# A transformer block on one core: output projection of all depth pairs as seven block products, weight sums from the prologue

## Chip, core and metric

The kernel runs on one core of a Trainium2 chip. Its engines are TensorE (PE; PEld is its weight load), VectorE (DVE), ScalarE (ACT), GpSimd (POOL) and SyncE (SP), which here only issues DMAs; each works through a queue of its own in the order of the program, and they wait for each other by semaphores. The metric is the device time of one execution in microseconds (us).

## The reference

One encoder block on x (1024 tokens by 1024, f32): a combined input projection, two groups of eight attention heads of width 64 (neighbourhood attention on a 16 x 64 grid with an 8 x 16 window and a relative bias; windowed attention with rotary positions, two key/value heads and a sink), SiLU gates, an output projection and a layer norm.

```python
h = jnp.einsum('bsd,de->bse', x, w_in[layer])
q_a, k_a, v_a, z_a, q_b, k_b, v_b, z_b = jnp.split(h, SPLIT_POINTS, axis=-1)
y_a = neighborhood_attention(q_a, k_a, v_a, rel_pos_bias[layer])
y_b = windowed_gqa_with_sink(rotary(q_b), rotary(k_b), v_b, sink_logits[layer])
mixed = jnp.concatenate([y_a * jax.nn.silu(z_a), y_b * jax.nn.silu(z_b)], axis=-1)
y = jnp.einsum('bse,ed->bsd', mixed, w_out[layer])
x = layer_norm(DEEPNORM_ALPHA * x + y, ln_gain[layer], ln_bias[layer])
```

## The kernel before

**Numbers.** Every operand of a product is held as two f16 tiles, hi and lo; a product is three passes, hi by hi, hi by lo, lo by hi. ScalarE makes hi (a scaled cast), VectorE or GpSimd makes lo (the source minus hi).

**Stages.** (1) Prologue, to about 60 us: v of both groups. A first half of the tokens is multiplied in f32 parts (line 551, eight depth steps; `load_wv` splits the weight, the last two steps' lo part on GpSimd, L510). `scales` (L573 to L584) then finds the scale `runit` of x and `unit` of the weight, by a chain of small VectorE operations. The second half of the tokens is done in f16: for each depth step k in the order `KO`, `ahead` lets ScalarE make the hi parts (L594 of the weight, L614 of x), VectorE the lo parts (`x16_part`, L615, and `wv_lo`, L598), three steps ahead of TensorE; two steps with the passes one after the other, the rest with all three passes of a matmul together. Steps take 2.45 us of TensorE. From the fourth on also the first half's x is split (`x16_part(0, k)`, again L615), which the input projection (`project`, L444) reads from 59.61 us on. Its weights are split by `w_split` (ScalarE L242, GpSimd L247 and L248). This part is written out in order by hand, so every queue has the order of the code. (2) Input projection and attention, to about 346 us: attention units with matmuls of the projection put between them, in step with a planner that gives the additional operations to GpSimd, ScalarE or VectorE by priority and estimated cost (`enq`, `fill_in`). Splits and sums of w_out and of the gated head outputs run here too. (3) Output projection and norm.

**The output projection.** The depth of 1024 is four pairs i = 0..3 of two 128-blocks, and the output tiles are taken as two halves of tokens (t and 4 + t) by two halves of columns. So there is a 2 x 2 by 2 x 2 block product for each pair. For pairs 0 and 1 (`NSP` = 2) it is done with seven products instead of eight, on sums S of the activations and T of the weights (`TERMS`: q1 = A11 B11, q2 = A12 B21, q3 = S4 B22, p4 = A22 T4, q5 = S1 T1, q6 = S2 T2, q7 = S3 T3). For pairs 2 and 3 it is eight plain products, appended to q2, q3, p4 and an eighth group d. The sums T of pairs 0 and 1 are made in stage 2 from loaded blocks of w_out (`t_prep`; `combine`, L1072 on GpSimd), split, and stored to a DRAM tile `td`, from which they are loaded when needed. Sums S come from `m_queue` and `m_split` (L1173, L1191).

**The end.** For each of four t, products are made into a PSUM bank and VectorE adds a bank to the f32 row tile `xr` (L1274; where the half row is complete, its statistics, L1280); `begin` and `finish` then take the row's mean and variance (L1284) and `norm` applies them. `norm` of tiles 0 to 2 and 4 to 6: ScalarE scales the whole row (L1346), GpSimd multiplies by the gain and adds the bias, in halves (L1348, L1349). Of tile 7 half is done by VectorE (L1339, L1343). The last tile is 3: its last product is cut in column blocks of 256, 128 and 128, and `norm_last` brings mean and deviation in through small matmuls (dm, L1311, and ds) while VectorE does the rest (L1315 to L1320). Warm-up matmuls without use (L1306) run between. GpSimd has nothing to do in the first half of the prologue but constants and L510.

**Heads.** As PSUM banks come free, the first closing products are put between the last attention units (`out_head`, `FILL_AT`, `FILL_N`), before all operands exist.

## Time and profile before

| | |
|---|---|
| time, median of 3 runs | 438.38 us (438.26 to 439.29) |
| the profiled execution: span from first to last instruction | 437.05 us |
| around the span, against the median | 1.33 us |
| granted TensorE clock | 1.000 |
| HBM read, written | 47.97 MB, 8.42 MB |
| prologue, to the first projection matmul | 59.61 us |
| first closing matmul (a head) | 346.05 us |
| last product ends, warm-up begins | 429.48 us |

The time of the profiled execution itself is its span of 437.05 us; the program's time has 1.33 us around it. Times in the rows are us from the start of the span. A row of a timeline has start, duration, engine, line of the program, operation, out<-in, and in brackets the idle time before it with what ended it; a row xN stands for N instructions in a run. A group has busy time, mean ns of one, idle time before.

### The profile page before, as it was taken

How to read it: one execution, taken by the hardware profiler on the slowest of the kernel's cores; microseconds unless marked ns; L12 is line 12 of the kernel's file. 1: busy time of each engine (PE TensorE's matmuls, PEld its weight loads, DVE VectorE, ACT ScalarE, POOL GpSimd, SP SyncE). 2: the span in 40 equal slices, each digit the busy share in tenths (PEclk: the TensorE clock that was granted, in tenths of full speed). 3: DMA queues.
4: the chain of work that ended last, by engine and by line, in shares of the span. 5: the costliest groups of instructions: out<-in, count | busy, mean ns of one | idle time of the engine just before them, and what ended most of it. 6: DMA issues, size and time to landing. Idle time of an engine off the chain costs nothing.

```text
span 437.0 us, 9409 instructions
## 1 busy us (share of the span) xinstructions
PE 431.1 (99%) x3225; PEld 253.3 (58%) x3225; DVE 337.6 (77%) x855; ACT 308.3 (71%) x663; POOL 275.6 (63%) x293
## 2 busy tenths in 40 slices
PE   9999999999999999999999999999999999999995
PEld 8997754444445656565656565565656555444444
DVE  5978976784878798888998898879887855575455
ACT  5749789768678979788988869887989743332321
POOL 0110073578428648778998899797899921068584
PEclk9999999999999999999999999999999999999999
DMA  8922479995429999997899999998999669711113
GB/s 265 406 92 61 119 242 324 255 291 175 128 56 196 207 181 205 163 191 129 153 190 215 189 204 191 226 196 159 182 191 247 118 125 370 300 48 73 73 73 121
DMA packets 128816, 80.09 MB, mean 183 GB/s; under 512 B 97280, under 2 KB 106368, under 8 KB 128768
## 3 DMA queue, kind: packets, MB, share of 16 engines
q1 hardware_dynamic: 128624, 79.36, 75.9%
q8 instruction: 25, 0.41, 0.4%
q14 instruction: 23, 0.19, 0.1%
q10 hardware_dynamic: 144, 0.13, 0.1%
HBM read 47.97 MB, written 8.42 MB: 129 GB/s over the span
## 4 chain that ended last, share of the span: by engine, by line
PE 79%; DVE 6%; ACT 6%; issue 4%; POOL 3%; DMA 1%; SPq 0%; DVEq 0%; ACTq 0%; POOLq 0%
PE ps_pj L444 39%; PE ps_s L1239 8%; PE ps_s L551 6%; PE ps_t L967 6%; PE ps_pj L1239 4%; PE ps_pj L551 3%; PE ps_t L551 3%; PE ps_s L890 3%; PE ps_s L891 3%; PE ps_t L1239 2%; POOL xr L1348 2%; POOL xr L1349 2%; DVE split L939 1%; ACT ps_s L920 1%; PE ps_t L1005 1%
## 5 line engine op out<-in xcount | busy, mean ns | idle before, releaser
L444 PE MATMUL ps_pj<-xf,wh 128*128 128x512 f16 x672 | 201.3, 379 | 0.0
L444 PE MATMUL ps_pj<-xf,wl 128*128 128x512 f16 x336 | 127.3, 379 | 0.0
L444 PEld LDWEIGHTS <-wh 128*128 128x128 f16 x672 | 63.7, 98 | 58.3
L920 ACT ACTIVATE ps_s<-sn,nm 128x321 f32<-128x321 f32 (+3 forms) x128 | 67.7, 529 | 33.4 <-DVE nm L904 32.3
L939 DVE SCALAR_TENSOR_TENSOR split<-ps_s,split 128x320 f16<-128x320 f32 (+2 forms) x128 | 62.7, 490 | 19.6 <-ACT split L938 18.3
L247 POOL TENSOR_SCALAR wr<-wr,wsc 128x512 f32<-128x512 f32 x32 | 22.9, 716 | 67.0 <-ACT wh L242 64.3
L938 ACT ACTIVATE split<-ps_s 128x320 f16<-128x320 f32 (+2 forms) x128 | 55.1, 430 | 1.7
L444 PEld LDWEIGHTS <-wl 128*128 128x128 f16 x336 | 32.8, 98 | 37.8
L248 POOL TENSOR_TENSOR wl<-wr,wh 128x512 f16<-128x512 f32 x32 | 40.3, 1260 | 2.7
L904 DVE CUSTOM_DVE_ANT_0 sn<-ps_s,bias,sg 128x368 f32<-128x368 f32 (+1 forms) x64 | 36.1, 565 | 3.5 <-PE ps_s L891 3.3
L904 DVE CUSTOM_DVE_ANT_0 sn<-ps_s,bm,nsk 128x320 f32<-128x320 f32 (+2 forms) x64 | 36.6, 572 | 2.6 <-PE ps_s L891 2.1
L890 PE MATMUL ps_s<-ks,qs 128*128 128x320 f16 (+3 forms) x128 | 38.2, 298 | 0.2 <-DVE split L939 0.2
L891 PE MATMUL ps_s<-ks,qs 128*128 128x320 f16 (+3 forms) x128 | 38.2, 298 | 0.0
L967 PEld LDWEIGHTS <-tr 128*128 128x128 f16 (+1 forms) x1056 | 36.2, 98 | 2.1 <-issue 0.4
L1239 PEld LDWEIGHTS <-m 128*128 128x128 f16 x198 | 19.0, 98 | 20.9 <-issue 0.2
L361 POOL COPY ks<-ks 64x512 f16<-64x512 f16 x40 | 25.9, 647 | 3.9 <-ACT ks L305 1.2
L1274 DVE SCALAR_TENSOR_TENSOR xr<-ps_s,yc,xr 128x512 f32<-128x512 f32 (+1 forms) x22 | 15.8, 724 | 13.8 <-PE ps_s L1239 13.5
L1346 ACT ACTIVATE xr<-xr,nmr,rstd 128x1024 f32<-128x1024 f32 x6 | 7.4, 1240 | 27.0 <-POOL nmr L1293 27.0
L1239 PEld LDWEIGHTS <-A 128*128 128x128 f16 x162 | 15.2, 98 | 15.7
L551 PEld LDWEIGHTS <-xf 128*128 128x128 f16 x192 | 18.6, 98 | 7.2
L242 ACT ACTIVATE wh<-wr,wsc 128x512 f16<-128x512 f32 x32 | 22.7, 709 | 0.0
L1348 POOL TENSOR_TENSOR xr<-xr,gb 128x512 f32<-128x512 f32 x13 | 16.9, 1302 | 8.1 <-ACT xr L1346 8.1
(223 smaller groups left out, 910.1 us busy)
## 6 DMA issues: line engine op xcount, KB each, us to landing
wr<-in_wt SPq DMA_DIRECT2D x32, 256.0 KB, 3.3
ws<-in_wt SPq DMA_DIRECT2D x15, 512.0 KB, 6.8
wor<-in_wo SPq DMA_DIRECT2D x20, 256.0 KB, 3.9
xr<-in_x SPq DMA_DIRECT2D x8, 512.0 KB, 10.4
out<-xr SPq DMA_DIRECT2D x15, 256.0 KB, 2.0
wob<-in_wo SPq DMA_DIRECT2D x14, 256.0 KB, 4.0
bias<-in_bias SPq DMA_DIRECT2D x8, 440.0 KB, 4.5
wvraw<-in_wv SPq DMA_DIRECT2D x9, 320.0 KB, 5.6
```

The costliest lines, as they stand in the source:

```text
L248: nc.gpsimd.tensor_sub(l, raw, h)
L361: nc.gpsimd.tensor_copy(place(t, o, half, col), place(t, a, half, col))
L444: nc.tensor.matmul(ps, a[:, k % 4, :], mv, start=(k == 0 and i == 0), stop=(k == KT - 1 and i == 2))
L551: nc.tensor.matmul(ps[:, :320], lh[:, ts], rh[:, cs], start=(k == ko[0] and i == 0), stop=(k == ko[-1] and i == 2))
L890: nc.tensor.matmul(ps[:, :n], q, sl[0], start=True, stop=False)
L891: nc.tensor.matmul(ps[:, :n], q, sl[1], start=False, stop=True)
L904: nc.vector.tensor_tensor_reduce(sn[:, at0:at0 + n], ps[:, :n], bias_t, sg[:, c:c + 1], init, op0=ALU.add, op1=ALU.min, accum_out=nm)
L920: nc.scalar.activation(pt[:, c], sn[:, c], AF.Exp, bias=nm, scale=-1.0, accum_out=acc)
L938: nc.scalar.activation(h, pt[:, c], AF.Copy, scale=PSCALE)
L939: nc.vector.scalar_tensor_tensor(l, pt[:, c], PSCALE, h, op0=ALU.mult, op1=ALU.subtract)
L967: nc.tensor.matmul(ps[:, w * m:w * m + e], a, b_, start=(i == 0), stop=(i == len(mms) - 1))
L1239: nc.tensor.matmul(ps[:, cs], lh[:, 128 * t:128 * t + 128], rh[:, cs], start=(fresh and e == 0 and n == 0), stop=(e == len(terms) - 1 and ...
```

## The change

It does all four depth pairs with the seven products and drops the plain ones (d, and the block B12). The sums T of all four pairs are made on GpSimd in the prologue: `t_load(i)` loads four 128 x 512 blocks of w_out into the tiles that held the f32 weight parts of v, `t_add(i)` makes four subtractions, `t_store(i)` stores the results in a DRAM tile `tf`. That is 4 MB more read and 4 MB more written in the prologue, all on SP's queue. `t_prep` in stage 2 loads tf, splits and stores, without subtractions; T of pairs 2 and 3 is loaded and split late (`t_late_load`, `t_late`), for which VectorE may take operations in the steps `LAST`. Sums S are made for pairs 2 and 3 too (`m_sums`, `m_last`). The heads have other lengths (`HEAD_N`: 9, 9, 6, 9, 9, 12, 12 matmuls instead of 12, 12, 6, 15, 18). The closing products have a new order; the last tile is 7, and its cut product is p4 with 12 matmuls a cut instead of q3 with 18. `norm` of every tile but the last is now split: ScalarE and GpSimd do half `ha`, VectorE does half `hb` with two operations (L1394, L1395 of the changed kernel). dm is made by ScalarE.

```diff
-NSP = 2
...
+T_KEYS = [("T1", 2), ("T1", 3), ("T2", 2), ("T2", 3), ("T3", 2), ("T3", 3), ("T4", 2), ("T4", 3)]
+T_SLOT = {"T1": 0, "T3": 1, "T4": 2, "T2": 3}
+T_AT, LAST = 122, range(129, 145)
...
+        wot = {}
+
+        def t_load(i):
+            for n in range(4):
+                t = vw.tile([128, 640], F32, tag=f"wv{'hl'[n % 2]}{2 * i + n // 2}", name="wot")
+                wot[i, n] = t[:, :512]
+                nc.sync.dma_start(wot[i, n], wo[i, :, n])
+
+        def t_add(i):
+            for o, a, b in ((0, 1, 0), (1, 3, 1), (3, 3, 0), (2, 2, 3)):
+                nc.gpsimd.tensor_sub(wot[i, o], wot[i, a], wot[i, b])
+
+        def t_store(i):
+            for n in range(4):
+                nc.sync.dma_start(tf[i, :, n], wot[i, n])
...
         nc.sync.dma_start(sk, sink)
+        t_load(0)
+        t_load(1)
+        t_add(0)
+        t_add(1)
...
+        t_store(0)
         wv_lo(KO[0])
         ahead(1)
         v_out(banks[4], 2, 0)
         ahead(2)
+        t_store(1)
+        t_load(2)
+        t_load(3)
+        t_add(2)
+        t_add(3)
...
+            if i == 5:
+                t_store(2)
...
         for i in range(4):
             sum_load(i)
+        t_store(3)
...
-    FILL_N = [48] * len(FILL) + [12, 12, 6, 15, 18]
+    FILL_N = [48] * len(FILL) + HEAD_N
...
-        def combine(o, a, b):
-            return enq("any", lambda eng: on_eng[eng].tensor_sub(wor[:, o], wor[:, a], wor[:, b]),
-                       *(t_sums[-1:] or [load_ops["wor", i, b] for b in range(4)]), prio=2, cost=SUM)
...
-        for n, t in ((0, t_sums[2]), (1, t_sums[1]), (3, t_sums[3]), (2, t_sums[3])):
+        for n in range(4):
+            t = enq("sp", lambda n=n: nc.sync.dma_start(wor[:, n], tf[i, :, n]), *([t_low[n]] if i else []))
...
+    def t_late_load(n, *deps):
+        key, i = T_KEYS[n]
+
+        def load():
+            t_raw[n] = wp.tile([128, 512], F32, tag="wr", name=f"tl{n}", bufs=5)
+            nc.sync.dma_start(t_raw[n], tf[i, :, T_SLOT[key]])
+
+        load_ops["tl", n] = enq("sp", load, *deps)
+
+    def t_late(n):
+        key = T_KEYS[n]
+
+        def hi():
+            if key not in part:
+                pair_of(big_ap([128, 2, 2, 512], F16, f"tp{n}"), *T_KEYS[n:n + 2])
+            nc.scalar.activation(part[key][0], t_raw[n], AF.Copy, scale=wsn)
+
+        o = enq("act", hi, load_ops["tl", n], prio=1.9, cost=0.65)
+        t_fin[n] = enq("any", lambda eng: lo_of(part[key][1], t_raw.pop(n), wsn, part[key][0], eng), o, prio=1.9, cost=LOW)
+        done[key] = [t_fin[n]]
...
-    NB = range(NSP, 4)
-    TERMS = {"q1": [("A11", "B11", n) for n in range(NSP)], "q6": [("S2", "T2", n) for n in range(NSP)],
-             "q5": [("S1", "T1", n) for n in range(NSP)], "q7": [("S3", "T3", n) for n in range(NSP)],
-             "q2": [("A12", "B21", n) for n in range(NSP)] + [(a, b, n) for n in NB for a, b in (("A11", "B11"), ("A12", "B21"))],
-             "q3": [("S4", "B22", n) for n in range(NSP)] + [(a, b, n) for n in NB for a, b in (("A11", "B12"), ("A12", "B22"))],
-             "p4": [("A22", "T4", n) for n in range(NSP)] + [(a, b, n) for n in NB for a, b in (("A21", "B11"), ("A22", "B21"))],
-             "d": [(a, b, n) for n in NB for a, b in (("A21", "B12"), ("A22", "B22"))]}
+    TERMS = {name: [(a, b, n) for n in range(4)] for name, a, b in (
+        ("q1", "A11", "B11"), ("q2", "A12", "B21"), ("q3", "S4", "B22"), ("p4", "A22", "T4"), ("q5", "S1", "T1"),
+        ("q6", "S2", "T2"), ("q7", "S3", "T3"))}
...
-            nc.gpsimd.tensor_scalar(dm, identf, mv[:, 0:1], -1.0, op0=ALU.mult, op1=ALU.mult)
+            nc.scalar.activation(dm, nident, AF.Copy, scale=mv[:, 0:1])
...
+            xr, ha, hb = xrs[t], slice(0, 512), slice(512, 1024)
             mv, sd = st_ or row_stats(t)
-            ha, hb = slice(0, 512), slice(512, 1024)
-            if t == 7:
-                nc.vector.scalar_tensor_tensor(xr[:, hb], xr[:, hb], mv[:, 0:1], gb[:, hb], op0=ALU.subtract, op1=ALU.mult)
-            rstd, nmr = row_scale(mv, sd, t == 7)
-            if t == 7:
-                nc.scalar.activation(xr[:, ha], xr[:, ha], AF.Identity, bias=nmr, scale=rstd)
-                nc.vector.scalar_tensor_tensor(xr[:, hb], xr[:, hb], rstd, bb[:, hb], op0=ALU.mult, op1=ALU.add)
-                nc.sync.dma_start(out[ts, hb], xr[:, hb])
-            else:
-                nc.scalar.activation(xr, xr, AF.Identity, bias=nmr, scale=rstd)
-            for h in (ha, hb)[:1 if t == 7 else 2]:
-                nc.gpsimd.tensor_mul(xr[:, h], xr[:, h], gb[:, h])
-                nc.gpsimd.tensor_add(xr[:, h], xr[:, h], bb[:, h])
-                nc.sync.dma_start(out[ts, h], xr[:, h])
+            rstd, nmr = row_scale(mv, sd)
+            nc.scalar.activation(xr[:, ha], xr[:, ha], AF.Identity, bias=nmr, scale=rstd)
+            nc.vector.scalar_tensor_tensor(xr[:, hb], xr[:, hb], mv[:, 0:1], gb[:, hb], op0=ALU.subtract, op1=ALU.mult)
+            nc.vector.scalar_tensor_tensor(xr[:, hb], xr[:, hb], rstd, bb[:, hb], op0=ALU.mult, op1=ALU.add)
+            nc.sync.dma_start(out[ts, hb], xr[:, hb])
+            nc.gpsimd.tensor_mul(xr[:, ha], xr[:, ha], gb[:, ha])
+            nc.gpsimd.tensor_add(xr[:, ha], xr[:, ha], bb[:, ha])
+            nc.sync.dma_start(out[ts, ha], xr[:, ha])
...
+        cb = [run("q5", t, bank("t"), range(3)) for t in range(2)]
+        q2(0, (3,))
+        add(1, 0, b[1])
+        q2(1, (3,))
+        q6(0)
+        for t in range(2):
+            run("q5", t, cb[t], (3,))
+            add(4 + t, 1, cb[t])
+        q7(0)
+        x_scale(2)
+        q3(0)
+        x_scale(6)
+        add(2, 0, b[2])
+        q6(1)
+        p4(0)
+        q5(2)
+        q7(1)
+        x_scale(3)
+        q3(1)
+        add(3, 0, b[3])
+        q6(2)
+        p4(1)
+        x_scale(7)
+        q5(3)
+        q7(2)
+        q2(2)
+        q3(2)
+        p4(2)
+        q6(3)
+        finish()
+        add(3, 1, run("q3", 3, cb[3]), whole=True)
+        q2(3)
+        run("q7", 3, b[3])
+        norm(3)
+        add(7, 1, b[3], whole=True)
+        norm_ahead(7)
+        add(7, 0, b[3])
         cuts = [((0, 256), bank("t")), ((256, 128), None), ((384, 128), None)]
         pn = bank("t")
         for c, ps in cuts:
             ps = ps or bank("pj" if c[0] == 256 else "s")
-            add(3, 1, run("q3", 3, ps, None, c), c, whole=True)
-        norm_last(3)
-
-    def m_last():
-        for n in ("A12", "A22"):
-            t = tiles["kq"].tile([128, 2, 512], F16, tag="ks", name=f"{n}_3", bufs=8)
-            part[n, 3] = t[:, 0], t[:, 1]
-        z = zt[ZP[3][1]]
-        for n, sl, eng in (("A12", ZL, "dve"), ("A22", ZH, "pool")):
-            m_split((n, 3), z[:, sl], low={eng: SUM[eng]})
-        need(*done["A12", 3], *done["A22", 3])
-
-    fill.extend((out_head((0,), range(4), "pj", "q2"), out_head((1,), range(4), "pj", "q2"),
-                 out_head((0, 1), (4,), None, "q2"), out_head((2,), range(5), "s", "q2"),
-                 out_head((0, 1, 2), range(2), "s")))
+            add(7, 0, run("p4", 3, ps, None, c), c, whole=True)
+        norm_last(7)
...
+    def m_last(between):
+        z, za = zt[ZP[3][1]], zt[ZP[3][0]]
+        need(*done["S3", 3])
+        for key in ("A12", "A22", "S1", "S2", "S4"):
+            m_home(key, 3)
+
+        def hi(key, src):
+            nc.scalar.copy(part[key, 3][0], src)
+
+        def lo(eng, key, src):
+            eng.tensor_sub(part[key, 3][1], src, part[key, 3][0])
+
+        hi("A12", z[:, ZL])
+        nc.vector.tensor_sub(za[:, ZL], z[:, ZH], za[:, ZL])
+        nc.gpsimd.tensor_add(za[:, ZH], za[:, ZH], z[:, ZH])
+        lo(nc.vector, "A12", z[:, ZL])
+        hi("S2", za[:, ZL])
+        hi("A22", z[:, ZH])
+        nc.vector.tensor_sub(z[:, ZL], z[:, ZL], za[:, ZL])
+        between()
+        lo(nc.vector, "S2", za[:, ZL])
+        lo(nc.gpsimd, "A22", z[:, ZH])
+        hi("S4", z[:, ZL])
+        lo(nc.vector, "S4", z[:, ZL])
+        hi("S1", za[:, ZH])
+        lo(nc.gpsimd, "S1", za[:, ZH])
```

GpSimd's queue in the prologue, from its last operation for v to its first splits of the projection weights; before:

```order
L510 TENSOR_TENSOR wvl_374<-wvraw,wvh_373 128x640
L510 TENSOR_TENSOR wvl_413<-wvraw,wvh_412 128x640
L247 TENSOR_SCALAR wr_520<-wr_520,wsc 128x512
L248 TENSOR_TENSOR wl_818<-wr_520,wh_817 128x512
L247 TENSOR_SCALAR wr_522<-wr_522,wsc 128x512
```

and of the changed kernel:

```order
L514 TENSOR_TENSOR wvl_375<-wvraw,wvh_374 128x640
L514 TENSOR_TENSOR wvl_414<-wvraw,wvh_413 128x640
L633 TENSOR_TENSOR wot<-wot 128x512 x16
L251 TENSOR_SCALAR wr_521<-wr_521,wsc 128x512
L252 TENSOR_TENSOR wl_883<-wr_521,wh_882 128x512
```

Sixteen subtractions (x16) stand between the lo parts of v's weight and the first split of a projection weight.

SP's queue from the last constant of the prologue on (sk is the sink); before:

```order
L231 DMA wr_528<-in_wt 128x512
L663 DMA bm<-in_bmask 128x320
L664 DMA sk<-in_sink 128x4
L591 DMA wvraw<-in_wv 128x640 x2
L604 DMA xraw_646<-in_xT 128x512
L604 DMA xraw_673<-in_xT 128x512
L604 DMA xraw_703<-in_xT 128x512
L604 DMA xraw_726<-in_xT 128x512
```

and of the changed kernel, from sk on:

```order
L684 DMA sk<-in_sink 128x4
L629 DMA wot<-in_wo 128x512 x8
L637 DMA tf<-wot 128x512 x4
L595 DMA wvraw<-in_wv 128x640 x2
L637 DMA tf<-wot 128x512 x4
L629 DMA wot<-in_wo 128x512 x8
L608 DMA xraw_703<-in_xT 128x512
L608 DMA xraw_730<-in_xT 128x512
L608 DMA xraw_760<-in_xT 128x512
L637 DMA tf<-wot 128x512 x4
L608 DMA xraw_787<-in_xT 128x512
```

The second loads of v's weight (wvraw) stand behind the first four stores, the second loads of x (xraw) behind eight stores and sixteen loads, one of them and the loads ws behind twelve stores; a store waits for its subtraction.

VectorE's queue near the end, around the norm of tile 7 before:

```order
L1280 BN_STATS stats_6037<-xr 128x6
L1274 SCALAR_TENSOR_TENSOR xr<-ps_s,yc,xr 128x512
L1280 BN_STATS stats_6037<-xr 128x6
L1284 BN_AGGR mv<-stats_6037 128x2
L1339 SCALAR_TENSOR_TENSOR xr<-xr,mv,gb 128x512
L1291 RECIPROCAL rstd<-sd 128x1
L1293 TENSOR_SCALAR nmr<-mv,rstd 128x1
L1343 SCALAR_TENSOR_TENSOR xr<-xr,rstd,bb 128x512
L1274 SCALAR_TENSOR_TENSOR xr<-ps_pj,yc,xr 128x512
```

and of the changed kernel, around the norm of tile 3, the one before the last:

```order
L1329 SCALAR_TENSOR_TENSOR xr<-ps_t,yc,xr 128x512
L1335 BN_STATS stats_6140<-xr 128x6
L1329 SCALAR_TENSOR_TENSOR xr<-ps_s,yc,xr 128x512
L1335 BN_STATS stats_6140<-xr 128x6
L1339 BN_AGGR mv<-stats_6140 128x2
L1346 RECIPROCAL rstd<-sd 128x1
L1348 TENSOR_SCALAR nmr<-mv,rstd 128x1
L1394 SCALAR_TENSOR_TENSOR xr<-xr,mv,gb 128x512
L1395 SCALAR_TENSOR_TENSOR xr<-xr,rstd,bb 128x512
L1329 SCALAR_TENSOR_TENSOR xr<-ps_s,yc,xr 128x512
L1335 BN_STATS stats_6185<-xr 128x6 x4
```

The two operations on SBUF halves that before stood only at tile 7 (xr<-xr,mv,gb and xr<-xr,rstd,bb) now stand in this way behind each of seven tiles, between additions from PSUM.

185 lines of the change are left out of this document (88 added, 97 removed).

## The prediction

> **What bounds the kernel now.** I read the page's busy shares first, then the waits of TensorE, then its chain of waits, then the timelines of single stretches. The busy shares and three rows of the page's slices:
>
> ```profile
> PE 431.1 (99%) x3225; PEld 253.3 (58%) x3225; DVE 337.6 (77%) x855; ACT 308.3 (71%) x663; POOL 275.6 (63%) x293
> ...
> PE   9999999999999999999999999999999999999995
> ...
> POOL 0110073578428648778998899797899921068584
> ...
> DMA  8922479995429999997899999998999669711113
> ```
>
> The waits of TensorE (what it waited for, total us, times, longest):
>
> ```profile
> PE ps_t L477 <- DVE warm L133: 1.0, 1, 1.0
> PE ps_t L1313 <- DMA out<-xr: 0.5, 1, 0.5
> PE ps_t L967 <- DVE z L992: 0.2, 1, 0.2
> PE ps_s L890 <- DVE split L939: 0.2, 1, 0.2
> ```
>
> TensorE waits 1.9 us in 437. Everything up to its last product is its own stream, so a matmul that goes is worth its pitch, and a wait that comes is paid in full. VectorE (DVE) and GpSimd (POOL) have spare time, but not everywhere: Each digit is the busy share of a slice of 10.9 us in tenths: GpSimd's idle slices are the 3rd to 5th (21.9 to 54.6 us) and those from 350 to 380 us. From the first of these the change takes its GpSimd time.
>
> **Part 1: fewer products.** In the chain of waits the pitch of the closing matmuls stands in one row (start, us, count):
>
> ```profile
> 401.00 10.37 PE ps_s L1239 x48
> ```
>
> 10.37/48 = 0.216 us for 512 columns. Per tile of 128 tokens the old terms are six per three-pass set: q1, q5, q6, q7 with 2 pairs (4 x 6 = 24), q2, q3, p4 with 2 + 4 terms (3 x 18 = 54) and d with 4 terms (12), 90 matmuls. New are seven products of 4 pairs by 3 passes, 84. Four tiles: 360 to 336, so 24 x 0.216 = **-5.2 us** of TensorE. The kept stages have no waits, so the eight POOL combinations that vanish from the attention stage (and two B splits) bring nothing themselves; it is their replacement that has a place of its own.
>
> **Part 2: sixteen subtractions on GpSimd in the prologue.** Before, GpSimd does nothing between two rows:
>
> ```profile
> 20.32 3.72 POOL L510 TENSOR_TENSOR wvl<-wvraw,wvh 128x640 fp32r<-128x640 f32 x2 [19.00 <-ACT wvh L507]
> 56.00 0.69 POOL L247 TENSOR_SCALAR wr<-wr,wsc 128x512 f32<-128x512 f32 x1 [31.96 <-ACT wh L242]
> ```
>
> and the same subtraction, in its old place, has this group:
>
> ```profile
> L1072 POOL TENSOR_TENSOR wor<-wor 128x512 f32<-128x512 f32 x8 | 10.2, 1272 | 0.4
> ```
>
> So 16 x 1.27 = 20.4 us fit into 32 us of idle GpSimd. The question is what they do to VectorE. Rows of the rotary part, where both engines work on SBUF (start, us):
>
> ```profile
> 110.60 0.68 DVE L381 TENSOR_TENSOR rp_sw<-rp_sw,sin 128x512 f32<-128x512 f32 x1
> 114.62 1.47 POOL L248 TENSOR_TENSOR wl<-wr,wh 128x512 f16<-128x512 f32 x1
> 115.00 1.64 DVE L381 TENSOR_TENSOR rp_sw<-rp_sw,sin 128x512 f32<-128x512 f32 x1
> 116.36 0.84 POOL L247 TENSOR_SCALAR wr<-wr,wsc 128x512 f32<-128x512 f32 x1 [0.27 <-ACT wh L242]
> 116.67 1.06 DVE L382 TENSOR_TENSOR rp_raw<-rp_raw,rp_sw 128x512 f32<-128x512 f32 x1
> ```
>
> Alone, L381 takes 0.68. At 115.00 it takes 1.64: it does its 0.68 after L248 has ended at 116.09. L247, issued at 116.36, waits for L381's end at 116.64 and ends at 117.20; L382, issued at 116.67, waits for that and ends at 117.73. The two engines take turns, whole instructions at a time. VectorE's operations in the prologue have the same two SBUF inputs:
>
> ```profile
> 28.28 0.15 DVE L580 TENSOR_TENSOR g<-g,least 32x2 f32<-32x2 f32 x1
> ...
> 35.02 0.75 DVE L615 SCALAR_TENSOR_TENSOR xf<-x,runit,xf 128x512 f16<-128x512 f32 x1 [1.36 <-ACT xf L614]
> 35.70 0.88 DVE L598 SCALAR_TENSOR_TENSOR wq<-wvraw,runit,wq 128x640 f16<-128x640 f32 x1
> 36.68 0.75 DVE L615 SCALAR_TENSOR_TENSOR xf<-x,runit,xf 128x512 f16<-128x512 f32 x1
> 37.35 0.88 DVE L598 SCALAR_TENSOR_TENSOR wq<-wvraw,runit,wq 128x640 f16<-128x640 f32 x1
> ...
> 57.94 0.92 DVE L615 SCALAR_TENSOR_TENSOR xf<-xraw,runit,xf 128x512 f16<-128x512 f32 x1
> ```
>
> and TensorE uses them at once (each of its eight steps takes 2.45 us; the third begins here):
>
> ```profile
> 38.37 0.57 PE L551 MATMUL ps_pj<-wq,xf 128*128 128x320 f16 x3
> ...
> 59.61 0.59 PE L444 MATMUL ps_pj<-xf,wh 128*128 128x512 f16 x2
> ```
>
> When do the subtractions come? The loads of wo stand behind these on SP; the page gives the time to landing of a load of that size:
>
> ```profile
> 18.09 3.00 SPq L231 DMA_DIRECT2D wr<-in_wt  x5
> ...
> 22.16 0.33 SPq L664 DMA_DIRECT2D sk<-in_sink  x1
> ```
> ```profile
> wr<-in_wt SPq DMA_DIRECT2D x32, 256.0 KB, 3.3
> ```
>
> At 0.6 us an issue the eight loads go out from 22.8 to 27.2 and land from about 27 to 31. A subtraction needs two tiles, so the first starts near 27.9, and GpSimd has eight in a row, 10.2 us if alone. Taking turns: L580 waits for the first (29.2 instead of 28.3). Subtractions 2 to 4 run beside small operations; then L615 and L598 of the first step, L615, L598 of the second and L615 of the third each let one through, 33.2 to 42.0, and the third step's L598 ends at 42.9 instead of 38.2. TensorE's third step then starts at 42.9 instead of 38.37: 4.5 us late. If loads land earlier or two of the pairings miss, one or two of the 1.27 us drop out; if VectorE always goes first, nothing is late. So 0 to 4.5; I take 3.2, the stepped value less one subtraction.
>
> The second eight wait on SP behind t_store(1), which waits for subtraction eight (41 us): 4 stores and 8 loads at 0.6 us, landing from about 46.5. They meet the last eleven L615/L598 up to the row at 57.94, which ended at 58.86 while its first reader (the tenth matmul of the projection, 59.61 + 9 x 0.216) came 2.9 us later. Eight subtractions are 10.2 us; maximum and scale operations and gaps of VectorE, which do not take part, hide 4 to 6. So 4 to 6 us of delay against 2.9 us of slack, which the first stall leaves as it is: 0 to 5, and I take 1.3, near the low end because GpSimd may run late instead. GpSimd cannot run much later, though: its own first split (56.00) waits for subtraction 16, and TensorE reads that split's lo half at 60.04 plus the delay. Sum of part 2: **+4.5** (0 to 9.5). The extra 8 MB themselves cost nothing: the DMA row of the slices shows 2, 2 and 4 tenths between 22 and 55 us; the x and ws loads that now stand behind the stores have several us to their readers.
>
> **Part 3: around the heads (346 to 372 us).** The order of TensorE is the same up to the first head. VectorE has spare time there, as the row before a late softmax scaling shows:
>
> ```profile
> 359.63 0.18 DVE L976 RECIPROCAL ri<-ps_t 128x4 f32<-128x4 f32 x1 [2.38 <-PE ps_t L967]
> ```
>
> A split of T and two splits of sums, three SBUF operations of 0.7 us each, now stand ahead of this reciprocal: 2.1 us into a gap of 2.38, less the time that GpSimd holds them up (one operation of 1.16, L248's length, at most). Between 0 and 1.5, I take one third of an operation: **+0.4**.
>
> **Part 4: the end.** Rows of VectorE at the end (start, us):
>
> ```profile
> 411.39 0.75 DVE L1274 SCALAR_TENSOR_TENSOR xr<-ps_s,yc,xr 128x512 f32<-128x512 f32 x1 [2.09 <-PE ps_s L1239]
> 412.18 0.69 DVE L1280 BATCH_NORM_STATS2 stats<-xr 128x6 f32<-128x512 f32 x1
> 412.79 0.15 DVE L1291 RECIPROCAL rstd<-sd 128x1 f32<-128x1 f32 x1
> ...
> 423.65 0.95 DVE L1339 SCALAR_TENSOR_TENSOR xr<-xr,mv,gb 128x512 f32<-128x512 f32 x1
> ...
> 424.84 1.44 DVE L1343 SCALAR_TENSOR_TENSOR xr<-xr,rstd,bb 128x512 f32<-128x512 f32 x1
> 426.20 0.74 DVE L1274 SCALAR_TENSOR_TENSOR xr<-ps_pj,yc,xr 128x512 f32<-128x512 f32 x1
> ...
> 430.47 0.37 DVE L1284 BATCH_NORM_AGGREGATE mv<-stats 128x2 f32<-128x48 f32 x1
> 430.88 0.75 DVE L1315 SCALAR_TENSOR_TENSOR xr<-xr,mv,gb 128x512 f32<-128x512 f32 x1
> ```
>
> An addition with its statistics takes 1.40 (411.39 to 412.79), an addition alone about 0.70. Before, six of eight norms cost VectorE only small operations. New, each norm puts two SBUF operations (0.75, start to start about 0.66, as L1315) on VectorE, beside GpSimd's multiply and add. From the end of q3 of tile 2 TensorE has 60 matmuls of 512, 12 of 256 and 24 of 128 columns left: 13.0 + 1.3 + 1.3 = 15.6 us. VectorE has behind that product: four additions with statistics (5.6), three additions alone (2.2), one statistics in four parts (0.8), three cuts of the last product with theirs (2.4), four aggregates (1.0), four reciprocals with nmr (1.2), together 13.2 us; and four norms of 1.32 alone (5.3), or, by the two rows at 423.65 and 424.84, which meet GpSimd's L1348 and L1349, at most 0.9 + 1.36 = 2.24 each (9.0). In the new order GpSimd's pair, 2.5 us, overlaps the next norm's first operation by some 0.5 us; I take 1.67 (6.7). So 19.9 against 15.6: VectorE becomes the bound there. TensorE, 5.2 earlier, ends q3 of tile 2 at 429.5 - 5.2 - 15.6 = 408.7 and VectorE's mean of the last tile is ready at about 409.1 + 19.9 = 429.0, the addition starting some 0.4 behind its product; it was 430.84. That is **-1.8** in place of -5.2 (-3.2 to +0.4 by the two bounds). The steps behind the mean are as before, dm on ScalarE may save 0.2, which I leave out.
>
> **Sum.** +4.5 + 0.4 - 1.8 = +3.1. The profiled execution spans 437.05, the median of the runs is 438.38, 1.33 more; 437.05 + 3.1 + 1.33 = 441.5.
>
> **Where the notes differ.** The Trainium skill, page "SBUF — State Buffer", section "Who interferes with whom", says that besides operations with two SBUF inputs also copy and tensor_scalar can enter modes that hold the pair of ports shared with GpSimd. For copies these rows agree (min/median/max ns: 228 alone, 1317 beside GpSimd); for small tensor_scalars they do not, L739 took 0.15 in the middle of a GpSimd operation:
>
> ```profile
> L751 DVE COPY vb<-vt x8: 228/229/1317, 68.1 to 82.3; 128x256 f16<-128x256 f16 x8
> ```
> ```profile
> 63.70 0.15 DVE L739 TENSOR_SCALAR vg<-vg 128x1 f32<-128x1 f32 x1
> ```
> ```profile
> 63.73 1.16 POOL L248 TENSOR_TENSOR wl<-wr,wh 128x512 f16<-128x512 f32 x1
> ```
>
> The chain of scales, L581 and four L583 behind L580, has two columns instead of one, so rows alone do not exclude that it waits.
>
> **Rivals.**
> - *VectorE keeps its pace in the prologue* (chance 0.27): it goes first whenever both are ready, or the subtractions fall into reduces and gaps, and GpSimd is the one that is late. For it: idle of 1.5 and 1.4 us before two L615. Against it: the turn at 116.36, and 10.2 us of GpSimd plus VectorE's L615/L598 do not fit before 38.2 from 27.9. It decides at a stall under about 1 us. Then 438.4 + 0.4 - 1.8 = 437.0, from 435.2 to 438.9 by the end's bounds: faster or no change.
> - *The whole gain* (0.10): also VectorE keeps up at the end because the order interleaves it better than I count, 438.4 - 5.2 = 433.2, up to 434.5.
> - *The scales wait as well* (0.13): each of five small operations behind L580 lets a subtraction through, runit comes up to 5 us later, of which 2 us are covered; 441.5 + 3 to 5, about 445.
>
> **How the numbers follow.** The forecast, stall of 2 to 7 us in the prologue, has 0.50 and gives 439.0 to 444.0, with some of the end's bounds 438.5 to 444.5. A measurement of this kernel tells about 0.3% (1.3 us) from no change. Faster: the whole gain 0.10, six tenths of the first rival 0.16, a small part of the forecast 0.04: 0.30. Same: the rest of the first rival 0.11 and 0.09 of the forecast: 0.20. Slower: 0.50. The range 434.5 to 446.0 leaves out most of the whole gain and the upper part of the last rival, under 0.2; the forecast's own range is 438.5 to 444.5.
>
> **What would show it.** Right: waits of TensorE on VectorE's lo splits between 33 and 50 us, VectorE's operations there 1.5 to 2.1 us long instead of 0.75 to 0.88, the first projection matmul at 63 to 66 instead of 59.61; in the end VectorE without idle from the q3 of tile 2 on, and warm matmuls starting earlier than the mean by more than 2 us. Wrong: the projection begins within 1 us of 59.61 (first rival), or VectorE waits for products up to the last cut (whole gain). The count of matmuls is certain, so a saving that is missing must show as idle time of TensorE.

## The result: slower, by about three times the forecast

| | before | changed |
|---|---|---|
| time, median | 438.6 us (438.26 to 439.29, 4 runs) | 449.5 us (448.2 to 452.57, 4 runs) |
| ratio of the times | | 1.0262, 95% interval 1.0221 to 1.0304 |
| profiled execution, span | 437.05 us | 446.4 us (its time 448.2) |
| last product ends | 429.48 us | 435.01 us |
| mean of the last tile ready | 430.84 us | 440.23 us |

The changed kernel is slower. Its 449.5 us lie outside the predicted range (434.5 to 446.0): the direction is right, the size is not. The profiled execution is 9.35 us longer than that of before, the medians differ by 10.9 us: the four runs spread more (448.2 to 452.6 us, with granted clocks of 0.992 to 0.985), and the profiled one is the fastest of them.

Busy shares and the clock row of the page of the changed kernel (tenths of full speed in 40 slices):

```profile
PE 428.9 (96%) x3189; PEld 249.8 (56%) x3189; DVE 357.4 (80%) x878; ACT 312.5 (70%) x676; POOL 292.5 (66%) x298
...
PEclk9999999999999999999999999999999999999996
```

TensorE has 36 matmuls less (18 whole ones, and six that were cut in three), as counted, but is busy 96% instead of 99%. What it waits for now (total us, times, longest):

```profile
PE ps_pj L1293 <- DVE xr L1329: 2.4, 1, 2.4
PE ps_t L1362 <- POOL xr L1354: 2.3, 1, 2.3
PE ps_pj L448 <- POOL wl L252: 1.6, 1, 1.6
PE ps_t L1368 <- ACT dm L1366: 1.2, 1, 1.2
PE ps_t L272 <- ACT junk L266: 1.0, 1, 1.0
...
PE ps_pj L555 <- DVE wq L602: 0.9, 2, 0.7
PE ps_s L923 <- DVE split L972: 0.8, 1, 0.8
PE ps_t L1000 <- DVE z L1025: 0.8, 1, 0.8
PE ps_s L555 <- DVE v L647: 0.8, 1, 0.8
```

Before, this view had four rows with 1.9 us in all. L555 and the wait of L448 for `wl` lie in the prologue, L272 at 94 us, L1000 and L923 in the attention, L1293 among the closing products, L1362 and L1368 behind the last product. To see what each costs, follow how much later than before the same instruction starts:

| instruction | before | changed | later by | added since |
|---|---|---|---|---|
| third matmul of the projection | 60.04 | 64.64 | 4.6 | 4.6 |
| `wm,ones` (L268, now L272) | 89.56 | 95.35 | 5.8 | 1.2 |
| last score matmul of the attention | 354.3 | 362.0 | 7.7 | 1.9 |
| last product, end | 429.48 | 435.01 | 5.5 | -2.2 |
| mean of the last tile, ready | 430.84 | 440.23 | 9.4 | 3.9 |
| span, end | 437.05 | 446.4 | 9.35 | 0.0 |

The -2.2 are 5.2 us of products that are gone, and 3.1 us of new waits at the closing products (2.6 at 383 us, 0.5 at 373 us).

**The prologue.** GpSimd's and VectorE's timeline of the changed kernel (start, us):

```profile
27.48 11.82 POOL L633 TENSOR_TENSOR wot<-wot 128x512 f32<-128x512 f32 x8 [4.06 <-DMA wot<-in_wo]
49.65 12.71 POOL L633 TENSOR_TENSOR wot<-wot 128x512 f32<-128x512 f32 x8 [10.35 <-DMA wot<-in_wo]
62.34 0.69 POOL L251 TENSOR_SCALAR wr<-wr,wsc 128x512 f32<-128x512 f32 x1
```
```profile
29.00 2.71 DVE L587 TENSOR_SCALAR unit<-g 32x2 f32<-32x2 f32 x4
...
33.42 1.25 DVE L619 SCALAR_TENSOR_TENSOR xf<-x,runit,xf 128x512 f16<-128x512 f32 x1 [1.51 <-ACT xf L618]
...
35.39 1.09 DVE L602 SCALAR_TENSOR_TENSOR wq<-wvraw,runit,wq 128x640 f16<-128x640 f32 x1
36.41 1.76 DVE L619 SCALAR_TENSOR_TENSOR xf<-x,runit,xf 128x512 f16<-128x512 f32 x1
38.09 1.89 DVE L602 SCALAR_TENSOR_TENSOR wq<-wvraw,runit,wq 128x640 f16<-128x640 f32 x1
39.90 0.74 DVE L619 SCALAR_TENSOR_TENSOR xf<-x,runit,xf 128x512 f16<-128x512 f32 x1
```

The first eight subtractions run back to back, and until GpSimd ends at 39.30 every lo part on VectorE takes 1.09 to 1.89 us instead of 0.75 to 0.88; behind that they are at their old length again, until the second eight begin. The second eight end at 62.3, and only then does GpSimd make its first split: TensorE's `wl` comes 1.6 us late.

**The end.** TensorE and VectorE of the changed kernel, from q3 of tile 2 on:

```profile
435.01 1.28 PE L1361 MATMUL ps_s<-warm 128*128 128x128 f16 x20
```
```profile
419.61 0.75 DVE L1329 SCALAR_TENSOR_TENSOR xr<-ps_t,yc,xr 128x512 f32<-128x512 f32 x1 [1.11 <-PE ps_t L1293]
...
421.32 0.74 DVE L1394 SCALAR_TENSOR_TENSOR xr<-xr,mv,gb 128x512 f32<-128x512 f32 x1
...
424.54 1.34 DVE L1394 SCALAR_TENSOR_TENSOR xr<-xr,mv,gb 128x512 f32<-128x512 f32 x1
425.91 1.64 DVE L1395 SCALAR_TENSOR_TENSOR xr<-xr,rstd,bb 128x512 f32<-128x512 f32 x1
...
439.86 0.37 DVE L1339 BATCH_NORM_AGGREGATE mv<-stats 128x2 f32<-128x48 f32 x1
```

VectorE has one wait of 0.42 us left between 419.61 and 440.23, 20.6 us; TensorE needs 15.6 us from the end of q3 (419.41) to its last product and has then to wait 5.2 us for the mean.

### The profile page after: what moved, and what is told of

It reads as the page before. It is cut to its first block, busy times and chain, and to the rows that moved or that the text cites. A ratio compares the mean times of both kernels' runs of the same rounds, so it can differ in the third digit from the quotient of the medians.

```text
span 446.4 us, 9462 instructions
## 1 busy us (share of the span) xinstructions
PE 428.9 (96%) x3189; PEld 249.8 (56%) x3189; DVE 357.4 (80%) x878; ACT 312.5 (70%) x676; POOL 292.5 (66%) x298
## 4 chain that ended last, share of the span: by engine, by line
PE 44%; DVE 19%; DMA 13%; ACT 10%; issue 8%; POOL 3%; SPq 2%; DVEq 0%; ACTq 0%; POOLq 0%
PE ps_pj L448 25%; PE ps_pj L1293 4%; PE ps_t L1000 4%; DMA vd<-vt 3%; PE ps_t L1293 3%; PE ps_s L1293 3%; DVE split L972 3%; DVE sn L937 3%; DMA wvraw<-in_wv 2%; PE ps_s L923 2%; PE ps_s L924 2%; POOL wot L633 2%; ACT ps_s L953 2%; DMA tl<-tf 2%; DMA T<-td 2%
## 5 line engine op out<-in xcount | busy, mean ns | idle before, releaser
L448 PE MATMUL ps_pj<-xf,wh 128*128 128x512 f16 x672 | 201.3, 379 | 0.0
L448 PE MATMUL ps_pj<-xf,wl 128*128 128x512 f16 x336 | 127.3, 379 | 1.6 <-POOL wl L252 1.6
L448 PEld LDWEIGHTS <-wh 128*128 128x128 f16 x672 | 63.8, 98 | 59.3 <-issue 1.3
L448 PEld LDWEIGHTS <-wl 128*128 128x128 f16 x336 | 32.9, 98 | 39.8 <-POOL wl L252 2.1
L923 PE MATMUL ps_s<-ks,qs 128*128 128x320 f16 (+3 forms) x128 | 38.2, 298 | 0.8 <-DVE split L972 0.8
L1000 PEld LDWEIGHTS <-tr 128*128 128x128 f16 (+1 forms) x1056 | 36.1, 98 | 2.7 <-issue 1.0
L633 POOL TENSOR_TENSOR wot<-wot 128x512 f32<-128x512 f32 x16 | 23.6, 1480 | 15.4 <-DMA wot<-in_wo 14.4
L1293 PEld LDWEIGHTS <-m 128*128 128x128 f16 x192 | 18.0, 98 | 22.2 <-issue 2.7
L1397 POOL TENSOR_TENSOR xr<-xr,gb 128x512 f32<-128x512 f32 x7 | 11.3, 1609 | 26.7 <-ACT xr L1393 26.7
L555 PEld LDWEIGHTS <-xf 128*128 128x128 f16 x192 | 18.6, 98 | 10.2 <-issue 3.0
L924 PEld LDWEIGHTS <-qs 128*128 128x128 f16 x128 | 12.5, 98 | 16.0 <-issue 1.5
L1393 ACT ACTIVATE xr<-xr,nmr,rstd 128x512 f32<-128x512 f32 x7 | 5.7, 813 | 22.2 <-DVE nmr L1348 22.2
```

The costliest lines, as they stand in the source:

```text
L448: nc.tensor.matmul(ps, a[:, k % 4, :], mv, start=(k == 0 and i == 0), stop=(k == KT - 1 and i == 2))
L633: nc.gpsimd.tensor_sub(wot[i, o], wot[i, a], wot[i, b])
L923: nc.tensor.matmul(ps[:, :n], q, sl[0], start=True, stop=False)
L924: nc.tensor.matmul(ps[:, :n], q, sl[1], start=False, stop=True)
L1000: nc.tensor.matmul(ps[:, w * m:w * m + e], a, b_, start=(i == 0), stop=(i == len(mms) - 1))
L1293: nc.tensor.matmul(ps[:, cs], lh[:, 128 * t:128 * t + 128], rh[:, cs], start=(fresh and e == 0 and n == 0), stop=(e == len(terms) - 1 and ...
```

## The experiments

All are timed in three rounds beside the kernel before, which had medians of 438.4 to 438.6 us there.

**The sums alone, and their transfers alone.** To the kernel before are added the loads, the subtractions and the stores of the prologue (`e1_before_sums`); the products stay as they were and the stored sums are not read. In `e2_before_moves` the subtractions are left out, and the raw blocks are stored. In `e3_after_nosubs` it is the changed kernel that lacks them, so that its T are raw blocks of w_out.

The edit of `e3_after_nosubs`:

```diff
         def t_add(i):
-            for o, a, b in ((0, 1, 0), (1, 3, 1), (3, 3, 0), (2, 2, 3)):
-                nc.gpsimd.tensor_sub(wot[i, o], wot[i, a], wot[i, b])
+            pass
```

> The kernel before with the prologue part of the change alone: the 16 loads of w_out blocks, the 16 subtractions on GpSimd and the 16 stores, at the places the change gives them; the results are not used, everything else is the kernel before. Theory (the two engines take turns at SBUF, and late loads follow): the first projection matmuls are 4 to 5 us late, the reads of the projection weight sums near 90 us 1 us more, so the span is 437 + 5 to 6 = 442 to 443. Rival 1 (the prologue costs little, the change loses its time at the end): 437 to 438.5. Rival 2 (the loss in the attention stage comes from here as well, by transfers that come late): 444 to 445.

> As the run with the prologue part alone, but without the 16 subtractions: loads and stores of w_out blocks only, the stored blocks are the raw ones and not used. Theory (the subtractions hold up VectorE's lo parts): the projection starts within 0.5 us of 59.6, the span is 437 to 438.5, and what it has over 437 is the wait near 90 us. Rival (transfers in SyncE's queue hold up the second loads of x and of v's weight): the projection starts 2 us late or more, span 440 to 443.

> The changed kernel without the 16 subtractions: the weight sums T are the raw blocks of w_out. Theory: TensorE is not late at the start of the projection, 4.6 us of the changed kernel's 446.4 go, span 441 to 442. If the wait near 90 us goes as well: 440.5. Rival (the prologue's delay is made up by later slack or returns as another wait): 444 to 446. The waits of the attention stage (1.0 us near 208 and 1.0 near 260) and the ones at the end (2.4 near 383, 3.9 behind the last product) stay by the theory.

Measured: 445.31 us (ratio 1.0159, 1.0135 to 1.0184), 439.98 us (1.002, 0.9997 to 1.0043) and 443.96 us (1.0142, 1.0107 to 1.0177). Waits of TensorE in the kernel before with the sums:

```profile
PE ps_pj L445 <- POOL wl L249: 1.7, 1, 1.7
PE ps_pj L552 <- DVE wq L599: 1.2, 2, 0.7
...
PE ps_s L552 <- DVE v L644: 0.8, 1, 0.8
...
PE ps_pj L552 <- DVE xf L616: 0.6, 1, 0.6
```

None of these rows is there with the transfers alone. So the 8 MB more cost between nothing and 1.9 us by the interval, and the subtractions 5.3 us (445.31 less 439.98): the prologue's part of the theory holds, in a kernel that has nothing else of the change. (The forecasts are spans, 442 to 443, 437 to 438.5 and 441 to 442; the traces have 443.8, 438.5 and 441.9, so the first is 0.8 too low.) But without the subtractions the changed kernel is still 5.5 us slower than the one before, although it has 5.2 us fewer products. So some 10.7 us, up to 1.9 of them by the transfers, are lost outside the sums, of which the prediction had 3.8 (3.4 at the end, 0.4 at the heads).

**Half of the sums.** As `e1_before_sums`, with only the first eight subtractions.

```diff
-            for o, a, b in ((0, 1, 0), (1, 3, 1), (3, 3, 0), (2, 2, 3)):
+            for o, a, b in ((0, 1, 0), (1, 3, 1), (3, 3, 0), (2, 2, 3))[:4 if i < 2 else 0]:
```

> The kernel before with the prologue part, of which only the first eight subtractions are left (pairs 0 and 1); loads and stores all stay. Theory (the first eight hold up the lo parts of the first steps, the second eight GpSimd's own first split): TensorE loses 2.5 to 3.5 us between 33 and 42 us and nothing near 63; span 441 to 442.5. Rival (either eight cost about the same, by total port time): 439.5 to 440.8.

Measured: 443.01 us (1.0095, 1.0067 to 1.0123). TensorE's gaps between 33 and 42 us (the time from start to start beyond the usual pitch) add up to 2.7 us (3.5 with all sixteen, 3.0 in the changed kernel), and the wait for `wl` at 63 us is gone. So the first eight cost 2.7 to 3.5 us, the second eight 1.7 us in TensorE's wait: the forecast had 3.2 and 1.3.

**What holds VectorE: reading or writing?** In the place of each subtraction, three memsets on GpSimd in the kernel before: it writes for as long, but reads nothing.

```diff
-                nc.gpsimd.tensor_sub(wot[i, o], wot[i, a], wot[i, b])
+                for _ in range(3):
+                    nc.gpsimd.memset(wot[i, o], 1.0)
```

> The kernel before with the loads and stores of the prologue part, and in place of each of the 16 subtractions three memsets of the same tile on GpSimd: GpSimd is busy in the same places and waits for the same loads, but reads no SBUF. Theory (VectorE's operations with two inputs and GpSimd's reads take turns): VectorE's lo parts keep their 0.75 and 0.88 us, the projection starts within 0.7 us of 59.6, span 438 to 439.5. Rival (any operation of GpSimd there holds VectorE up, or the waits between the queues do): the projection 2 us late or more, span 441 to 444.

Measured: 442.21 us (1.0084, 1.0056 to 1.0112). GpSimd and VectorE:

```profile
27.19 13.11 POOL L631 MEMSET wot<- 128x512 f32 x24 [3.34 <-DMA wot<-in_wo]
```
```profile
29.41 2.21 DVE L584 TENSOR_SCALAR unit<-g 32x2 f32<-32x2 f32 x4
...
33.33 0.75 DVE L616 SCALAR_TENSOR_TENSOR xf<-x,runit,xf 128x512 f16<-128x512 f32 x1 [1.51 <-ACT xf L615]
...
34.80 0.88 DVE L599 SCALAR_TENSOR_TENSOR wq<-wvraw,runit,wq 128x640 f16<-128x640 f32 x1
```

Beside 13 us of memsets the operations with two SBUF inputs keep 0.75 and 0.88 us, so it is GpSimd's reading that holds them up. The tensor_scalars of the scales do not keep their length: four of them took 0.68 us before, and take 2.21 us here and 2.71 us beside the subtractions. This is what the Trainium skill states, page "SBUF — State Buffer", section "Who interferes with whom", and the prediction set aside on the row of L739, which has 128x1. By the Trainium skill, page "VectorE: DVE Perf Modes", section "Mode 2×_2P — use both read ports for one tensor", such a mode needs an outermost dimension longer than one that is even (or odd and alike in source and destination), which 32x2 has and a single column has not. The measurements agree with both. The row of L739 shows less than the prediction read from it: it starts at 63.70, 0.03 us ahead of GpSimd's operation, not in the middle of one. Rows of the changed kernel do show it: four tensor_scalars of 128x1 between 50.23 and 50.88 us take 0.15 to 0.20 us each, while GpSimd's first subtraction of the second eight runs until 51.26.

The time of this run lies between the theory and its rival: the profiled execution spans 441.3 us (438 to 439.5 by the theory). The scales alone make `runit` 2.0 us late, the projection begins at 60.65 instead of 59.61, and GpSimd's first split, which stands behind the memsets, holds TensorE up for 1.3 us more.

**The same sums behind the prologue.** Half of them on VectorE, from 65 us on, with three edits of experiments below in it (casts, pools, norm share).

```diff
+            at(26 + 7 * n, t_add, n // 4, n % 4, nc.gpsimd)
+            at(29 + 7 * n, t_add, 2 + n // 4, n % 4, nc.vector)
```

> The changed kernel with the casts and the pools mended (the norm as changed), and the 16 subtractions moved behind the prologue: loads as in the changed kernel, eight subtractions on GpSimd and eight on VectorE, one every 1.5 us between the matmuls of the first projection (65 to 77 us), stores there too. Theory (the place of the subtractions is what costs, not their number): TensorE is not late at 59.6 us, the splits that the projection needs have slack of several us there; span 439 to 440.5, against 446.4 less 1.2 and 1.2 with the subtractions in the old place. Rival (GpSimd's splits of projection weights, or v's parts, are now late): 442 to 445.

Measured: 457.99 us (1.0443, 1.042 to 1.0467), the slowest of all. The prologue has no gap, but the operations of the projection are late instead:

```profile
PE ps_pj L448 <- POOL wl L252: 8.5, 1, 8.5
PE ps_t L272 <- ACT junk L266: 4.9, 1, 4.9
```

TensorE's stream has no slack there either, and the granted clock is 0.50 for 3.4 us behind the wait of 4.9 us and for 10.2 us around the one of 8.5 us (see the last section). As the edits are mixed in this kernel, the shares of the sums and of the pools in these 13.4 us are not separated.

**The wait at 94 us.** L272 waits for a reduction on ScalarE. ScalarE is held up by a copy `rp_raw` of the rotary part (L382), which waits 4.1 us for stores `vd<-vt`. The full diff, beyond the excerpt shown, takes these scratch tiles (tag `va`) from another pool, `kq` instead of `ap`; there they come to lie on the v tiles, whose stores must end first. The experiment makes this move alone, in the kernel before (the line below, and the two like it for the other tiles of this tag).

```diff
-        raw = tiles["ap"].tile([128, 1024], F32, tag="va", name="rp_raw", bufs=6)[:, :512]
+        raw = tiles["kq"].tile([128, 1024], F32, tag="va", name="rp_raw", bufs=6)[:, :512]
```

> The kernel before with one part of the change: the scratch tiles named va (the rotary's raw and swapped tiles, the gathered v, the biases) are taken from the pool kq instead of ap, nothing else. Theory (the first rotary tile then lies on v tiles that are still being stored, and ScalarE waits for those stores): a wait of TensorE of 1 to 1.6 us for the weight sums (L268) near 88 us, ScalarE's L378 there with an idle time ended by the stores of v; span 438 to 438.7. Rival (that wait belongs to the prologue's extra transfers): no wait there, 437 to 437.3.

Measured: 439.66 us (1.003, 1.0012 to 1.0048, ten runs). ScalarE and the waits of TensorE in it:

```profile
89.09 0.60 ACT L378 ACTIVATE rp_raw<-ps_pj 128x512 f32<-128x512 f32 x1 [5.63 <-POOL wl L248]
```
```profile
PE ps_t L268 <- ACT junk L262: 1.7, 1, 1.7
```

and the same instruction in the changed kernel (without the subtractions it waits 4.10 us for the same stores):

```profile
94.09 0.60 ACT L382 ACTIVATE rp_raw<-ps_pj 128x512 f32<-128x512 f32 x1 [4.12 <-DMA vd<-vt]
```

In the kernel before this copy begins at 85.87, with the product that it reads. The move alone brings a TensorE wait of 1.7 us to the kernel before, whose view of waits had none there, and from the third matmul of the projection to the last score matmul this trace takes 1.6 us more (295.9 instead of 294.3). So that the move causes the wait is shown. What the copy waits for is read from the views, which name the last of several things: a store in the changed kernel, GpSimd's split in this run.

**The wait at 383 us.** q7(0) needs the bank that VectorE's addition (0, 1) reads. Rows of ScalarE, VectorE and TensorE of the changed kernel:

```profile
375.26 1.06 ACT L1324 ACTIVATE xr<-xr 128x1024 f32<-128x1024 f32 x1 [5.26 <-DMA xr<-in_x]
376.22 0.60 ACT L1505 CAST A<-z 128x512 f16<-128x512 f32 x1
```
```profile
376.86 0.69 DVE L1508 TENSOR_TENSOR A<-z,A 128x512 f16<-128x512 f32 x1 [1.58 <-ACT A L1505]
...
384.95 0.73 DVE L1329 SCALAR_TENSOR_TENSOR xr<-ps_pj,yc,xr 128x512 f32<-128x512 f32 x1
```
```profile
385.74 1.46 PE L1293 MATMUL ps_pj<-T,m 128*128 128x512 f16 x6 [2.43 <-DVE xr L1329]
```

The addition ends at 385.68, and q7(0) starts at 385.74. The casts for the last sums stand on ScalarE behind the scaling of x, which waits for its load. The experiment puts them ahead of it.

```diff
-        x_scale(0)
...
-        m_last(lambda: add(0, 0, b[0]))
+        m_last(lambda: (x_scale(0), add(0, 0, b[0])))
```

> The changed kernel with one order changed on ScalarE: the scaling of row tile 0 of x, which waited 5.3 us for its load, stands behind the first three casts of the last pair's sums instead of ahead of them. Theory (those casts stand behind a late load, and so VectorE reaches the addition that TensorE's q7 of tile 0 waits for 1.6 us late): the wait of 2.4 us near 383 shrinks to about 1, span 1 to 1.6 less than the changed kernel's 446.4 if the end follows, 444.8 to 445.4. Rival (VectorE's own two-input operations beside GpSimd's make the wait, not the casts): 446 to 446.6, no change.

Measured: 448.31 us (1.0234, 1.0191 to 1.0277), against 449.5 us; the two intervals overlap. The wait before q7(0) falls from 2.59 to 1.61 us (start to start beyond the usual pitch). But q6(0), ahead of it, now starts 0.4 us late, because the addition of tile 0 comes later in this order, so the stretch loses 2.0 us instead of 2.6. By this one trace about a quarter of the loss is the order on ScalarE; the rest stands in VectorE's own queue, which in this trace is busy from 382.24 up to the addition without a pause, and ahead of that has a lo part and a sum of 1.74 and 1.54 us instead of 0.69:

```profile
379.00 1.74 DVE L1507 TENSOR_TENSOR A<-z,A 128x512 f16<-128x512 f32 x1
380.78 1.54 DVE L1515 TENSOR_TENSOR z<-z,z 128x512 f32<-128x512 f32 x1
```

That GpSimd's share of those last sums is the rest of the cause is read from this, not tested by itself.

**The end: less of the norm on VectorE.** Of each row VectorE does 256 columns instead of 512, ScalarE and GpSimd 768.

```diff
-            xr, ha, hb = xrs[t], slice(0, 512), slice(512, 1024)
+            n = 512 if t == 3 else 768
+            xr, ha, hb = xrs[t], slice(0, n), slice(n, 1024)
```

> The changed kernel, with another share of the norm of tiles 0 to 2 and 4 to 6: VectorE does 256 columns instead of 512, ScalarE and GpSimd 768 instead of 512 (GpSimd in pieces of 384). Theory (VectorE is the bound from q3 of tile 2 on, 20.6 us of work beside 15.6 of TensorE): three of the four norms in that stretch lose 2 x 0.33 us each and meet GpSimd more often, the mean of the last tile is ready 1.5 to 2 us earlier against TensorE's last product (5.2 us behind it before, 3.2 to 3.7 now), span 444.4 to 445. Rival (GpSimd's longer work holds VectorE up as much as it saves, or the end waits for GpSimd): 446 or more.

Measured: 448.77 us (1.0233, 1.0198 to 1.0268). VectorE's stretch from q3 of tile 2 to the mean is 20.5 us (418.87 to 439.35), as long as before the edit (20.6). The halved operations of the first of these norms take 0.48 us; those of the next two do not:

```profile
423.26 0.89 DVE L1395 SCALAR_TENSOR_TENSOR xr<-xr,mv,gb 128x256 f32<-128x256 f32 x1
424.19 1.10 DVE L1396 SCALAR_TENSOR_TENSOR xr<-xr,rstd,bb 128x256 f32<-128x256 f32 x1
...
426.26 1.13 DVE L1395 SCALAR_TENSOR_TENSOR xr<-xr,mv,gb 128x256 f32<-128x256 f32 x1
```

GpSimd, which has half more columns, is busy then, and VectorE waits for a turn. What it saves in columns it pays in turns: the rival of this experiment was right.

**The end: the norm as before.** ScalarE and GpSimd do whole rows, and the addition and the statistics of tile 7 go before norm(3).

```diff
+            nc.scalar.activation(xr, xr, AF.Identity, bias=nmr, scale=rstd)
+            for h in (slice(0, 512), slice(512, 1024)):
+                nc.gpsimd.tensor_mul(xr[:, h], xr[:, h], gb[:, h])
+                nc.gpsimd.tensor_add(xr[:, h], xr[:, h], bb[:, h])
```

> The changed kernel with the norm of tiles 0 to 6 as before the change (ScalarE scales the whole row, GpSimd multiplies and adds in two halves, VectorE nothing), GpSimd's part of the last tile ahead of the norm of tile 3. Theory (VectorE is the bound in the end because of these norms): from the addition of q3 of tile 2 to the mean of the last tile VectorE needs 17 instead of 20.6 us, bound by TensorE again, the mean is ready 1.4 to 2 us behind the last product (5.2 before); but GpSimd has 5.1 us a tile for the four last norms, and the span ends with it: 445.5 to 448. Rival (VectorE is late for another reason): the mean stays 4 us or more behind the last product.

Measured: 453.77 us (1.0347, 1.0282 to 1.0412). VectorE now waits for products again, and GpSimd ends last:

```profile
432.96 0.75 DVE L1329 SCALAR_TENSOR_TENSOR xr<-ps_t,yc,xr 128x512 f32<-128x512 f32 x1 [1.48 <-PE ps_t L1293]
```
```profile
428.34 1.26 POOL L1395 TENSOR_TENSOR xr<-xr,gb 128x512 f32<-128x512 f32 x1 [5.13 <-ACT xr L1393]
...
449.33 1.32 POOL L1396 TENSOR_TENSOR xr<-xr,bb 128x512 f32<-128x512 f32 x1
```

From 428.34 to 450.65 GpSimd does not pause. The mean comes 3.5 us behind the last product (440.59 and 444.07) instead of 5.2, between the theory (1.4 to 2) and its rival (4 or more), but norms are left over. The two operations on VectorE were the price of not having that. (Up to the last score matmul this trace lost 3.7 us more than that of the changed kernel, and 1.8 us more among the closing products, where the clock fell, so its total is not the price of the norm alone.)

**All repairs together.** Norm share, casts first, and two pools of the prologue in the other order, so that the scratch tiles come to lie elsewhere (`e6_mended`); and that without subtractions, T being raw blocks (`e7_mended_nosubs`).

```diff
-        vp = vctx.enter_context(tc.tile_pool(name="vp", bufs=2))
         vw = vctx.enter_context(tc.tile_pool(name="vw", bufs=1))
+        vp = vctx.enter_context(tc.tile_pool(name="vp", bufs=2))
```

> The changed kernel with three mends together: the norm's share as in the run with another share of the norm; the casts of the last pair ahead of the scaling of row tile 0; and the two pools of the prologue opened in the other order, so that the rotary's first scratch tile no longer lies where the v tiles are that must still be stored. Theory: the wait near 94 us (1.2) goes, it was that ScalarE operation's wait for the stores of v and not a full queue; the one near 383 is halved (1.2); the end gains 1.5 to 2; span 441.5 to 442.5. Rival (the wait near 94 comes from transfers being late in general): it stays, 443 to 444.

> The kernel with three mends, without the 16 subtractions: T is the raw blocks of w_out. If the losses found so far add up, 4.5 us less than with them: 437 to 438, that is, the kernel before's time, with the 5.2 us of matmuls given back at the end (about 2 to 3), around the heads (about 1) and in the attention stage (about 1). Rival (something else holds the kernel, the mends do not add): 439 to 441.

Measured: 451.71 us (1.0297, 1.0273 to 1.0322) and 447.15 us (1.0197, 1.0159 to 1.0234). Both miss. The wait at 94 us is gone, but other tiles lie on the v tiles now, and GpSimd waits for the same stores (the longest TensorE wait of `e6_mended`, and GpSimd's row behind it):

```profile
PE ps_pj L448 <- POOL wl L252: 5.1, 2, 4.0
```
```profile
99.27 0.74 POOL L863 MEMSET split<- 128x768 f16 x1 [5.97 <-DMA vd<-vt]
```

Around this wait the granted clock is 0.50 for 6.8 us, from about 101.6 to 108.4. So the repair moved the wait to where it costs more, and whether the losses simply add up could not be tried with these two. Only the price of the subtractions held: 4.6 us between these two runs, 5.3 in the kernel before, 5.5 in the changed kernel. No version was faster than the kernel before.

## Why the prediction was right in direction and wrong in size

- **Part 1, the products: right.** 36 matmuls less, 5.2 us; from the end of q3 of tile 2 to the last product TensorE takes 15.6 us (419.41 to 435.01), the figure of the prediction.
- **Part 2, the prologue: right, +4.5 predicted, +4.6 in the trace.** The subtractions cost 5.3 us in the kernel before, and the transfers have no wait to show. Both halves are near their values (3.2 and 1.3 predicted; the projection's first matmul is 2.85 us late, the third another 1.75). That the sum fits to 0.1 us is luck: without subtractions the third matmul starts at 60.04 and 60.14 us in two traces and at 58.98 and 58.99 in two others. And two parts of the way there were not as told. The four small operations L583 (now L587) let subtractions through as well, so `runit` is 2.1 us late, as the third rival had it, at a chance of 0.13; but a subtraction let through there is not let through later, so the sum stayed and the 445 us of that rival did not follow from it. And the second eight cost TensorE nothing through VectorE's lo parts, although these take up to 1.63 us there: GpSimd was the late one, through its own first split, which the text had named only as a limit. The 1.3 of this half fits by luck.
- **Part 3, the heads: small, as said, but for another reason.** A gap of 0.5 us at 373 us waits for a load of T, not for the reciprocal, so that 0.4 was predicted is luck.
- **Part 4, the end: right as a mechanism, a little short.** VectorE is the bound: 20.6 us instead of 19.9 from the addition of q3 to the mean, and the mean comes 3.9 us later against the last product than before, where 3.4 were predicted. The four norms took 7.3 us instead of 6.7, because one met GpSimd twice (1.34 and 1.64). But -1.8 became +1.7, because of the next point but one.
- **The step that failed: "The kept stages have no waits, so the eight POOL combinations that vanish from the attention stage (and two B splits) bring nothing themselves".** The sum took from it that nothing changes between the prologue and the heads. There 3.1 us were lost. 1.2 come from scratch tiles that moved to another pool, so that a copy waits, by the views for the stores of the tiles below it; that the move does it is shown by `e9_va_in_before`. The diff has this move, the prediction gives it no term. The other 1.9 are small waits in the attention, 0.97 us at 208 us and 1.01 us at 259 us in the first place, which are 0.40 and 0.38 before; these two make 1.2 of the 1.9. The first is also 0.96 in the kernel with only transfers, but it is not there in `e12_first_eight`, which has the same transfers, nor in the changed kernel without subtractions, which loses as much in this stage (297.6 us from the third matmul of the projection to the last score matmul, 297.4 in the changed kernel, 294.3 before). The second was found in the traces of the changed kernel with and without sums. The cause of these 1.9 us stays open.
- **The second step that failed: the closing products as a mere stream up to q3 of tile 2.** The prediction let TensorE reach that point "5.2 earlier", and looked for VectorE's debts only behind it. The new order has a first debt at 383 us, 2.6 us, where the last sums, a wait for x and five additions meet; about a quarter is ScalarE's order (`e4_casts_first`), the rest is read from VectorE's queue and not tested by itself.
- **The difference of the medians.** The profiled execution has 1.8 us around its span; the median is 1.3 us above that execution. See the clock, below.

In numbers, by the trace: 4.6 + 1.2 + 1.9 + 3.1 - 5.2 + 3.9 = 9.5, against 9.35 in the spans. The prediction had 4.5 + 0.4 - 5.2 + 3.4 = 3.1. What it priced came to within 0.5 us each; 5.7 us (1.2, 1.9 and 2.6) were not priced at all.
